# First values kind by kind, softplus on GpSimd, and four tables of a two-layer trunk a tick later

## The chip, the core and the metric

The kernel runs on one core of a Trainium2 chip. A core has five engines that run side by side, each with its own stream of instructions: TensorE (PE) multiplies matrices, VectorE (DVE) works on vectors, ScalarE (ACT) evaluates functions and copies, GpSimd (POOL) does small work and issues some transfers, and SyncE (SP) issues the others. They are tied by semaphores: an instruction waits until what it reads is written. The metric is the device time of one execution in microseconds (us). Lower is better.

## What is computed

Two layers, each with a residual sum and a LayerNorm, on 512 tokens of width 1024, all in float32. The first ("even") layer feeds two branches from one input projection; the second ("odd") is differential attention. Cut to its steps, the reference is:

```python
# even layer
q, k, v, g_ret, xb, g_lru = split(x @ w_in)
q, k = rope(q), rope(k) * 128 ** -0.5
ret = retention(q, k, v)                     # 8 heads of 128, causal, decaying per head
ret = group_norm(ret) * gn_g + gn_b          # per head
ret = ret * silu(g_ret)
xc = causal_conv4(xb) + conv_b
r, i = sigmoid(xc @ wa + ba), sigmoid(xc @ wx + bx)     # 8 diagonal blocks of 128
log_a = -8 * r * softplus(-lam)
h = scan(a=exp(log_a), u=xc * i * sqrt(1 - exp(2 * log_a)))
y = concat(ret, h * silu(g_lru)) @ w_out
x = layer_norm(alpha * x + y)
# odd layer, 8 heads of two maps each
p = softmax(causal(q @ k.T))                 # rope on q and k; 16 maps
o = (p[map 0] - lam * p[map 1]) @ v          # values 256 wide
o = o * rsqrt(mean(o ** 2) + eps) * subln_g * (1 - lambda_init) * silu(g)
x = layer_norm(alpha * x + o @ w_out)
```

## The kernel before

Every operand of a large product is held as two parts, a high half and a low half: ACT casts the float32 value to the matmul's type (`h`), and DVE subtracts that from the value to get the rest (`l`). `split` (L146) does both. A product is three matmuls, here called kinds: high by high, high by low, low by high (`mm3`, L155). Each is 128 by 128 by up to 512 columns, and sums into a bank of PSUM. Weights come through `fetch` (L171): SP issues the transfer of 128 rows by 1024 columns into a raw buffer, which is then split; the names in the profile are `w0_r`, `w0h`, `w0l` and so on, numbered in the order of use. The raw buffers are few, so a later transfer waits until an earlier split is done.

PE and SP run in the order in which the program is written. The order on ACT, DVE and POOL is made by a scheduler when the kernel is built; `tc.high_priority(n)` raises an instruction by `n`, and `keep_in_program_order` pins one.

The program is a row of large units (values, gates, queries and keys, output), whose matmuls fill PE. Beside them run small jobs: the retention of a head, a block of the recurrence, a block of 128 queries of attention, LayerNorm. Each is a generator. After each triple of matmuls the large unit calls `side.tick()`; a job that has yielded `n` goes on `n` ticks later, and then puts its own few matmuls into PE's stream. The tables at the top of the program (L28 to L38) hold these delays. `RET_SCORES` and `RET_NORM` are those of a head of retention before its next score block and before its group norm, `LRU_GATES` that of a block of the recurrence before its gates, `ATT_TURN` that of attention between the transposes of its weights and their product with the values, by block of queries, and `ATT_NORM` that between this product and the transposes of its normalised result `o`.

These are the places that the change touches, and what stands there.

- *The first unit*, `v_even(0)` through `s_unit` (L206): the values of the first half of the heads, in four blocks of 128 tokens (`sb`), each with its own bank (`ev_ps`), over 8 slices of the contraction (`kt`), two to each of the weights w0 to w3. Block by block it does the three kinds of one slice, then of the other; for w0 it does all blocks of the first slice ahead of the second. x itself arrives in pieces, split by ACT and DVE (`xh`, `xl`), and w0 in two halves. A filler matmul on constants (L320) stands behind the very first one. When the last slice of a block is done, `evac` (L450) takes the mean of each head off: a reduce, a small scaling and a subtract on DVE (L454, L455, L457), then a split. The next unit, `gl0`, begins in the bank of block 0.
- *Softplus* (L422 to L440): 23 steps on 128 by 8 numbers, one of them a reciprocal, all on DVE. The result (`sp`) is first read by ACT in the gates of block 0 of the recurrence (L535).
- *A head of retention* (L467): four score blocks (`rs`), each multiplied by the decay (`rsd`) and split (`r00h` and so on: head, block), then their product with the values (`ro`), its square (`rq`), and the sum of it over the head by ones (`rv`). The score blocks have a priority of `P_SCORES` = 13, the rotation of queries and keys (`rope`, L343) one of `P_ROPE` = 50.
- *Attention* (L645): scores (`as`), mask and maximum on DVE (`nm`), exponential on ACT (`e`, L658), transposes (`wt`), split (`w33h`: head and block), the product with the values (`po`), its sum of squares on ACT (L691), the root on GpSimd (L694, L363), `o` on DVE (L697), transposes of it back into the same bank (L701), and a split (`om`). The product takes a bank of its own or borrows one of the large units; `own` says which. While a unit of gates and values runs, `busy[0]` is 1; while a query or key unit runs, `spare[0]` is set.
- *A unit of gates and values* (`gates_values`, L777) uses four banks, `one` (`gv2a` in the second such unit) and `two` (`gv2b`). It multiplies into `one`, then into `two`; half way through the latter, ACT copies `one` out (L799, names `p`), and the unit goes on summing into `one` (L156, right operand `sx`).

## Time and profile before

| | us |
|---|---|
| median of 3 runs | 925.92 (925.37 to 926.28) |
| the profiled execution, its own time | 926.56 |
| span of its profile | 924.8 |
| PE busy | 907.1 (98%) |
| DVE busy | 743.9 (80%) |
| ACT busy | 478.1 (52%) |
| POOL busy | 104.5 (11%) |

The granted clock of TensorE is 0.997 of full speed. Matmuls are pipelined: one of 512 columns is drawn 0.39 us long, and the next begins 0.23 us after it. So a pause of PE is read from the start of one matmul to the start of the next. A wait view gives for each engine what it waited for, in all, how often, and the longest; a row of a timeline gives start, length, engine, line, operation and operands, and in brackets the idle time ahead of it with its releaser.

### The profile page before, as it was taken

The numbers are of one execution on the slowest core, as the hardware profiler recorded it, in microseconds if no ns is written. First come the engines' busy times: TensorE is split into PE (matmuls) and PEld (weight loads), VectorE is DVE, ScalarE is ACT, GpSimd is POOL, SyncE is SP. The second block draws the span as 40 slices with busy tenths as digits, with TensorE's granted clock in tenths as the row PEclk, the third lists the DMA queues.
The fourth block names the chain that finished last, engine by engine and source line by source line (L and its number), as shares of the span: only waits on it lengthen the run. The fifth ranks groups of instructions, "written<-read, shape, count | busy, mean of one in ns | idle before, by whom it ended". The sixth has DMA issues, their size and how long they took to land.

```text
span 924.8 us, 11823 instructions
## 1 busy us (share of the span) xinstructions
PE 907.1 (98%) x4257; PEld 750.3 (81%) x4257; DVE 743.9 (80%) x1244; ACT 478.1 (52%) x779; POOL 104.5 (11%) x167
## 2 busy tenths in 40 slices
PE   8999999999999999999999999999999999999996
PEld 6888888888888878888888888888888888788885
DVE  5977987959768988897888897759868678868787
ACT  5567787557474668532424456433456333664340
POOL 0120010110102010010101210000120100201122
PEclk9999999999999999999999999999999999999998
DMA  7895463862929371534842226546237382277102
GB/s 251 276 314 150 122 169 108 261 183 58 289 57 280 92 193 61 179 117 151 331 167 69 69 68 246 210 163 245 72 130 253 141 318 87 74 258 265 48 1 91
DMA packets 46522, 152.92 MB, mean 165 GB/s; under 512 B 6144, under 2 KB 6272, under 8 KB 45696
## 3 DMA queue, kind: packets, MB, share of 16 engines
q1 hardware_dynamic: 41472, 135.39, 41.4%
q0 software_dynamic: 4992, 16.78, 9.4%
q8 instruction: 33, 0.54, 0.2%
q14 instruction: 25, 0.20, 0.1%
HBM read 139.57 MB, written 37.75 MB: 192 GB/s over the span
## 4 chain that ended last, share of the span: by engine, by line
PE 73%; DVE 14%; ACT 5%; issue 3%; POOL 3%; DMA 1%; SPq 0%; DVEq 0%; ACTq 0%; POOLq 0%
PE oo_ps L159 2%; PE oo_ps L156 2%; PE oo_ps L158 2%; PE out_ps L156 2%; PE out_ps L159 2%; PE out_ps L158 2%; ACT e L658 1%; PE gr_ps L159 1%; PE gr_ps L158 1%; PE gr_ps L156 1%; PE gl_ps L156 1%; PE gl_ps L159 1%; PE gl_ps L158 1%; POOL ave L694 1%; DMA w_r<-in_ev_w 1%
## 5 line engine op out<-in xcount | busy, mean ns | idle before, releaser
L658 ACT ACTIVATE e<-as,nm 128x128 f32<-128x128 f32 (+3 forms) x64 | 33.2, 524 | 42.5 <-DVE nm L655 42.4
L697 DVE SCALAR_TENSOR_TENSOR o<-po,ars,og 128x256 f32<-128x256 f32 x32 | 15.5, 484 | 36.5 <-POOL ars L363 36.4
L665 POOL TENSOR_SCALAR zr<-z 128x1 f32<-128x1 f32 x32 | 14.9, 466 | 259.2 <-ACT e L658 259.2
L187 POOL DMA_DIRECT2D t<-t x24 | 18.8, 784 | 159.0 <-DMA t<-in_od_w 154.6
L187 POOL DMA_DIRECT2D t<-in_od_w x24 | 19.0, 792 | 146.5 <-DMA t<-in_od_w 146.5
L694 POOL TENSOR_SCALAR ave<-ss,zr 128x1 f32<-128x1 f32 x32 | 17.9, 559 | 133.9 <-ACT po L691 133.2
L655 DVE CUSTOM_DVE_ANT_0 as<-as,mask 128x128 f32<-128x128 f32 (+3 forms) x64 | 30.3, 510 | 1.4 <-PE as L159 1.4
L691 ACT ACTIVATE po<-po 128x256 f32<-128x256 f32 x32 | 11.9, 373 | 30.9 <-PE po L159 30.8
L536 DVE TENSOR_TENSOR xbp<-xbp,xc 128x512 f32<-128x512 f32 x8 | 5.5, 691 | 18.4 <-ACT xbp L533 18.4
L363 POOL TENSOR_TENSOR ars<-ave,nhalf 128x1 f32<-128x1 f32 x32 | 19.5, 608 | 2.7
L666 DVE SCALAR_TENSOR_TENSOR e<-e,zr,e 128x128 f32<-128x128 f32 (+3 forms) x32 | 17.6, 550 | 0.8
L519 DVE SCALAR_TENSOR_TENSOR xc<-xbp,vecs,xc 128x509 f32<-128x509 f32 (+2 forms) x24 | 17.9, 747 | 0.1
L262 DVE TENSOR_TENSOR y<-oo_ps,y 128x512 f32<-128x512 f32 x24 | 16.0, 685 | 2.2 <-PE oo_ps L159 2.1
L475 DVE TENSOR_TENSOR rsd<-rs,dec 128x512 f32<-128x512 f32 (+3 forms) x32 | 15.6, 488 | 2.7 <-PE rs L159 2.7
L363 POOL TENSOR_TENSOR lrs<-lve,nhalf 128x1 f32<-128x1 f32 x8 | 7.3, 909 | 84.4 <-DVE lve L376 84.4
L701 PEld LDWEIGHTS po<-ident,o 128*128 128x128 f32 x64 | 8.6, 141 | 7.3 <-DVE o L697 3.8
L701 PE MATMUL po<-ident,o 128*128 128x128 f32 x64 | 12.5, 276 | 1.8 <-DVE o L697 1.8
L670 PE MATMUL wt<-ident,e 128*128 128x128 f32 x80 | 13.9, 272 | 0.0
L528 ACT ACTIVATE t<-pr,vecs 128x512 f32<-128x512 f32 x8 | 5.5, 688 | 15.8 <-PE pr L159 15.8
L663 DVE RECIPROCAL zr<-z 128x1 f32<-128x1 f32 x32 | 5.2, 162 | 10.3 <-ACT e L658 9.9
L670 PEld LDWEIGHTS wt<-ident,e 128*128 128x128 f32 x80 | 10.5, 141 | 3.5
L152 ACT CAST hh<-ht 128x512 fp32r<-128x512 f32 x8 | 4.7, 586 | 15.8 <-PE ht L615 15.8
(2846 smaller groups left out, 3474.5 us busy)
## 6 DMA issues: line engine op xcount, KB each, us to landing
w_r<-in_od_w SPq DMA_DIRECT2D x58, 512.0 KB, 5.6
w_r<-in_ev_w SPq DMA_DIRECT2D x47, 512.0 KB, 5.4
t<-in_od_w SPq DMA_DIRECT2D x48, 256.0 KB, 5.8
sx<-sd SPq DMA_DIRECT2D x24, 512.0 KB, 5.7
w_r<-t SPq DMA_DIRECT2D x24, 512.0 KB, 3.3
w_r<-in_ev_wo SPq DMA_DIRECT2D x16, 512.0 KB, 5.3
w_r<-in_od_wo SPq DMA_DIRECT2D x16, 512.0 KB, 4.0
t<-in_od_w POOLq DMA_DIRECT2D x24, 256.0 KB, 5.0
```

The lines of the kernel that those rows point to most:

```text
L156: nc.tensor.matmul(out=out, lhsT=l[0], rhs=r[0], start=start, stop=False, **kw)
L158: nc.tensor.matmul(out=out, lhsT=l[0], rhs=r[1], start=False, stop=False, **kw)
L159: nc.tensor.matmul(out=out, lhsT=l[1], rhs=r[0], start=False, stop=stop, **kw)
L187: nc.gpsimd.dma_start(out=dst, in_=two, max_dma_last_dim=4 * D, accum_op=ALU.add)
L363: nc.gpsimd.tensor_tensor(out=out, in0=var, in1=nhalf[:, :1], op=ALU.pow)
L519: nc.vector.scalar_tensor_tensor(out=xc[:, sh:], in0=xb[:, :S - sh], scalar=conv_w(w, c), in1=xc[:, sh:], op0=ALU.mult, op1=ALU.add)
L655: nc.vector.tensor_tensor_reduce(out=ps[:, :n], in0=ps[:, :n], in1=mask[:, S - n:], scale=-QK_SCALE, scalar=3.0e38, op0=ALU.add, op1=ALU.m ...
L658: nc.scalar.activation(out=e, in_=ps[:, :n], func=AF.Exp, scale=-1.0, bias=nm, accum_out=z[:, mp:mp + 1])
L666: nc.vector.scalar_tensor_tensor(out=ee[0], in0=ee[1], scalar=zr[:, 0:1], in1=ee[0], op0=ALU.mult, op1=ALU.add)
L670: nc.tensor.transpose(out=pt[:, kb * P:kb * P + P], in_=ee[0][:, kb * P:kb * P + P], identity=ident)
L694: nc.gpsimd.tensor_scalar(out=ve, in0=ss, scalar1=zr[:, 1:2], scalar2=None, op0=ALU.add)
L701: nc.tensor.transpose(out=pm[:, i * P:i * P + P], in_=o[:, i * P:i * P + P], identity=ident)
```

## The change

The first four weights (w0 to w3) are multiplied kind by kind: for a slice, one kind for all four blocks, then the next kind. The filler matmul is gone. The first half of w0 is cast by DVE and not by ACT. All of softplus but the reciprocal moves from DVE to GpSimd, with the last step cut in two. The last score block of a head gets the priority `P_SQUARE` = 60, above the rotation. Heads 1 and 3 wait one tick more before their group norm, block 2 of the recurrence one more before its gates, the last block of queries one more before its product with the values. Between this product and the transposes of `o`, one tick more is waited for where `spare[0]` is set; elsewhere the delay is `ATT_NORM + busy[0]`.

```diff
@@ -27,12 +27,12 @@
 
 RET_START = (13, 13, 13, 13, 13, 13, 13, 8)
 RET_SCORES = (4, 4, 4, 7)
-RET_NORM = (8, 6, 8, 6, 8, 6, 5, 5)
-LRU_GATES = (12, 12, 12, 12, 12, 12, 9, 12)
+RET_NORM = (8, 7, 8, 7, 8, 6, 5, 5)
+LRU_GATES = (12, 12, 13, 12, 12, 12, 9, 12)
 LN_TURN = 15
 ATT_START, ATT_GAP = (12,) * 7 + (7,), (8,) * 7 + (7,)
 ATT_SCORES = (7, 7, 7, 9)
-ATT_TURN = (4, 3, 4, 4)
+ATT_TURN = (4, 3, 4, 5)
 ATT_NORM = 5
 ATT_VALUE, GV_VALUE = 2, 4
 ATT_FREE, ATT_LENT = 2, 8
@@ -143,20 +143,18 @@
     def cut(t, *ix):
         return t[0][ix], t[1][ix]
 
-    def split(src, dst, scale=None):
+    def split(src, dst, scale=None, copy=nc.scalar.copy):
         if scale is not None:
             s = sg[:, scale:scale + 1]
             nc.scalar.activation(out=dst[0], in_=src, func=AF.Identity, scale=s)
             nc.vector.scalar_tensor_tensor(out=dst[1], in0=src, scalar=s, in1=dst[0].bitcast(F32), op0=ALU.mult, op1=ALU.subtract)
             return
-        nc.scalar.copy(out=dst[0], in_=src)
-        nc.vector.tensor_tensor(out=dst[1], in0=src, in1=dst[0].bitcast(F32), op=ALU.subtract)
-
-    def mm3(out, l, r, start, stop, between=lambda: None, **kw):
-        nc.tensor.matmul(out=out, lhsT=l[0], rhs=r[0], start=start, stop=False, **kw)
-        between()
-        nc.tensor.matmul(out=out, lhsT=l[0], rhs=r[1], start=False, stop=False, **kw)
-        nc.tensor.matmul(out=out, lhsT=l[1], rhs=r[0], start=False, stop=stop, **kw)
+        copy(out=dst[0], in_=src)
+        return nc.vector.tensor_tensor(out=dst[1], in0=src, in1=dst[0].bitcast(F32), op=ALU.subtract)
+
+    def mm3(out, l, r, start, stop, kinds=range(3), **kw):
+        for n in kinds:
+            nc.tensor.matmul(out=out, lhsT=l[n == 2], rhs=r[n == 1], start=start and n == 0, stop=stop and n == 2, **kw)
 
     def load(name, shape, src, pl=None, tag=None, bufs=None):
         t = (pl or const).tile(shape, F32, tag=tag or name, name=name, bufs=bufs)
@@ -177,7 +175,7 @@
             for lo, hi in parts:
                 c = slice(lo, hi)
                 nc.sync.dma_start(out=raw[:, c], in_=src[:, c])
-                split(raw[:, c], cut(w, ALL, c), scale=scale)
+                split(raw[:, c], cut(w, ALL, c), scale=scale, copy=nc.vector.tensor_copy if n == 0 and lo == 0 else nc.scalar.copy)
                 yield
             for then in behind.pop(n, ()):
                 then()
@@ -204,13 +202,13 @@
         return ps
 
     def s_unit(act, name, major, evac, before=None):
-        def product(ps, w, sb, kt):
+        def product(ps, w, sb, kt, kinds=range(3)):
             j = kt % 2 * HALF
-            between = {"between": lambda: busy_pe(2)} if (taken[0], sb, kt) == (1, 0, 0) else {}
-            mm3(ps, cut(act, ALL, kt, slice(sb * P, sb * P + P)), cut(w, ALL, slice(j, j + HALF)), kt == 0, kt == KT - 1, **between)
-            if kt == KT - 1:
-                evac(sb, ps)
-            side.tick()
+            mm3(ps, cut(act, ALL, kt, slice(sb * P, sb * P + P)), cut(w, ALL, slice(j, j + HALF)), kt == 0, kt == KT - 1, kinds)
+            if 2 in kinds:
+                if kt == KT - 1:
+                    evac(sb, ps)
+                side.tick()
 
         if major:
             with tc.high_priority(P_WEIGHTS):
@@ -224,12 +222,16 @@
             ps = [bank(ps_pj, "pj", f"{name}_ps{sb}") for sb in range(SB)]
             for i in range(KT // 2):
                 w = take(2)
-                steps = [(sb, j) for sb in range(SB) for j in range(2)]
-                if taken[0] == 1:
-
-                    steps.sort(key=lambda t: t[1])
-                for sb, j in steps:
-                    product(ps[sb], w, sb, 2 * i + j)
+                if taken[0] <= KT // 2:
+
+                    for j in range(2):
+                        for n in range(3):
+                            for sb in range(SB):
+                                product(ps[sb], w, sb, 2 * i + j, (n,))
+                    continue
+                for sb in range(SB):
+                    for j in range(2):
+                        product(ps[sb], w, sb, 2 * i + j)
 
     def out_unit(mix, y, name, first, before=None, after=None, late=0, early=0, apart=False):
         n = len(mix)
@@ -328,13 +330,15 @@
     halves = fetch(((0, HALF), (HALF, D)))
     for n, (lo, hi) in enumerate(((0, 1), (1, 2), (2, 4), (4, 6), (6, 8))):
         nc.sync.dma_start(out=xr[:, lo:hi], in_=a["xt"][:, lo:hi])
+        if n == 0:
+            next(halves)
         for kt in range(lo, hi):
-            split(xr[:, kt], cut(x, ALL, kt))
-        if n < 2:
-            next(halves)
-            if n == 1:
-                list(halves)
-        elif n < 4:
+            low = split(xr[:, kt], cut(x, ALL, kt))
+            if n == 0:
+                tc.keep_in_program_order(low)
+        if n == 1:
+            list(halves)
+        elif 1 < n < 4:
             list(fetch())
 
     nhalf = const.tile([P, SB], F32, tag="nhalf", name="nhalf")
@@ -426,18 +430,19 @@
     lam = vecs[:, 7]
     nc.scalar.activation(out=sa, in_=lam, func=AF.Abs)
     nc.scalar.activation(out=sa, in_=sa, func=AF.Exp, scale=-1.0)
-    nc.vector.tensor_scalar(out=sb_, in0=sa, scalar1=2.0, scalar2=None, op0=ALU.add)
+    nc.gpsimd.tensor_scalar(out=sb_, in0=sa, scalar1=2.0, scalar2=None, op0=ALU.add)
     nc.vector.reciprocal(out=sb_, in_=sb_)
...
-    nc.vector.scalar_tensor_tensor(out=sp4, in0=sb_, scalar=4.0, in1=sc, op0=ALU.mult, op1=ALU.add)
+        nc.gpsimd.tensor_tensor(out=sc, in0=sc, in1=sb_, op=ALU.mult)
+        nc.gpsimd.tensor_scalar(out=sc, in0=sc, scalar1=1.0 / n, scalar2=None, op0=ALU.add)
...
+    nc.gpsimd.tensor_scalar(out=sb_, in0=sb_, scalar1=4.0, scalar2=None, op0=ALU.mult)
+    nc.gpsimd.tensor_tensor(out=sp4, in0=sb_, in1=sc, op=ALU.add)
 
     def silu(ps, out, name):
         s = work(name + "_sg")
@@ -470,7 +475,7 @@
             n = S - jb * P
             ps = bank(ps_sc, "sc", f"rs{h}{jb}")
             mm3(ps[:, :n], cut(k, ALL, slice(jb * P, jb * P + P)), cut(q, ALL, slice(jb * P, S)), True, True)
-            with tc.high_priority(P_SCORES):
+            with tc.high_priority(P_SCORES if jb < SB - 1 else P_SQUARE):
                 s = temp(f"rsd{h}{jb}")
                 nc.vector.tensor_tensor(out=s[:, :n], in0=ps[:, :n], in1=dec[:, :n], op=ALU.mult)
                 t = part(n, f"r{h}{jb}")
@@ -695,7 +700,7 @@
             rsqrt(ve, rs)
             o = es.tile([P, 2 * P], F32, tag="o", name=f"o{hd}{qb}")
             nc.vector.scalar_tensor_tensor(out=o, in0=po[:, :2 * P], scalar=rs, in1=gates[qb, hd // 2][:, hc:hc + 2 * P], op0=ALU.mult, op1=ALU.mult)
-        yield ATT_NORM + max(not own, busy[0])
+        yield ATT_NORM + max(1 + (not own) if spare[0] else 0, busy[0])
         pm = po[:, 2 * P:]
         for i in range(2):
             nc.tensor.transpose(out=pm[:, i * P:i * P + P], in_=o[:, i * P:i * P + P], identity=ident)
```

The order of the instructions shows it at three places. On PE, at the beginning of the first V unit, the order was this (the names are bank, weight, and part of x; `ev_ps_245` and on are the banks of the four blocks):

```order
L156 MATMUL ev_ps_245<-w0h,xh 128x512
L321 MATMUL idle<-ones 128x256
L158 MATMUL ev_ps_245<-w0l,xh 128x512
L159 MATMUL ev_ps_245<-w0h,xl 128x512
L156 MATMUL ev_ps_246<-w0h,xh 128x512
L158 MATMUL ev_ps_246<-w0l,xh 128x512
L159 MATMUL ev_ps_246<-w0h,xl 128x512
L156 MATMUL ev_ps_247<-w0h,xh 128x512
```

and now it is this, with the banks `ev_ps_246` to `_249`:

```order
L157 MATMUL ev_ps_246<-w0h,xh 128x512
L157 MATMUL ev_ps_247<-w0h,xh 128x512
L157 MATMUL ev_ps_248<-w0h,xh 128x512
L157 MATMUL ev_ps_249<-w0h,xh 128x512
L157 MATMUL ev_ps_246<-w0l,xh 128x512
L157 MATMUL ev_ps_247<-w0l,xh 128x512
L157 MATMUL ev_ps_248<-w0l,xh 128x512
L157 MATMUL ev_ps_249<-w0l,xh 128x512
L157 MATMUL ev_ps_246<-w0h,xl 128x512
L157 MATMUL ev_ps_247<-w0h,xl 128x512
L157 MATMUL ev_ps_248<-w0h,xl 128x512
L157 MATMUL ev_ps_249<-w0h,xl 128x512
```

The three kinds of one bank stood together; now each kind runs over the four banks before the next one begins.

On DVE, behind the first V unit, the group means of the four blocks stood apart, with the split of w6 and of the values themselves between them:

```order
L153 TENSOR_TENSOR w4l<-w_r,w4h 128x1024
L153 TENSOR_TENSOR w5l<-w_r,w5h 128x1024
L454 TENSOR_REDUCE vm<-ev_ps_245 128x4
L455 TENSOR_SCALAR vm<-vm 128x4
L457 TENSOR_TENSOR vc<-ev_ps_245,vm 128x512
L454 TENSOR_REDUCE vm<-ev_ps_246 128x4
L153 TENSOR_TENSOR w6l<-w_r,w6h 128x1024
L153 TENSOR_TENSOR ev00l<-vc,ev00h 128x512
L455 TENSOR_SCALAR vm<-vm 128x4
L454 TENSOR_REDUCE vm<-ev_ps_247 128x4
```

and now stand together behind w6:

```order
L153 TENSOR_TENSOR w5l<-w_r,w5h 128x1024
L153 TENSOR_TENSOR w6l<-w_r,w6h 128x1024
L459 TENSOR_REDUCE vm<-ev_ps_246 128x4
L459 TENSOR_REDUCE vm<-ev_ps_247 128x4
L460 TENSOR_SCALAR vm<-vm 128x4
L153 TENSOR_TENSOR gw0l<-gw_437,gw0h 128x512
L460 TENSOR_SCALAR vm<-vm 128x4
L462 TENSOR_TENSOR vc<-ev_ps_246,vm 128x512
L462 TENSOR_TENSOR vc<-ev_ps_247,vm 128x512
L459 TENSOR_REDUCE vm<-ev_ps_248 128x4
```

The subtract of block 0 (`vc` of the first bank), which frees the bank, stood directly behind its own reduce and scaling; now a second reduce, a second scaling and the split `gw0l` stand between.

On ACT, in the second unit of gates and values, the two copies out of `gv2a` stood ahead of the cast of w117 and of the next head's exponentials (`e`):

```order
L152 CAST w116h<-w_r 128x1024
L691 ACTIVATE po_6188,ss<-po_6188 128x256
L799 COPY p_6215<-gv2a_6099 128x512
L799 COPY p_6217<-gv2a_6100 128x512
L152 CAST w117h<-w_r 128x1024
L658 ACTIVATE e_6235,z<-as_6229,nm 128x128
L658 ACTIVATE e_6243,z<-as_6237,nm 128x128
L774 ACTIVATE p_6215<-og_6272 128x512
```

and now stand behind them, the second one behind `om3h` too:

```order
L152 CAST w116h<-w_r 128x1024
L696 ACTIVATE po_6179,ss<-po_6179 128x256
L152 CAST w117h<-w_r 128x1024
L663 ACTIVATE e_6222,z<-as_6216,nm 128x128
L663 ACTIVATE e_6230,z<-as_6224,nm 128x128
L804 COPY p_6237<-gv2a_6099 128x512
L152 CAST om3h<-po_6179 128x2x128
L804 COPY p_6239<-gv2a_6100 128x512
L152 CAST w33h<-wt_6260 128x512
```

The square of `po` keeps its place behind w116h; the copies have moved past the cast of w117 and two exponentials.

More of the change, by code (lines that the diff above doesn't have):

```diff
@@ L428, in trunk @@
     nc.scalar.activation(out=sa, in_=sa, func=AF.Exp, scale=-1.0)
-    nc.vector.tensor_scalar(out=sb_, in0=sa, scalar1=2.0, scalar2=None, op0=ALU.add)
+    nc.gpsimd.tensor_scalar(out=sb_, in0=sa, scalar1=2.0, scalar2=None, op0=ALU.add)
     nc.vector.reciprocal(out=sb_, in_=sb_)
-    nc.vector.tensor_tensor(out=sa, in0=sa, in1=sb_, op=ALU.mult)
-    nc.vector.tensor_tensor(out=sb_, in0=sa, in1=sa, op=ALU.mult)
-    nc.vector.tensor_scalar(out=sc, in0=sb_, scalar1=1.0 / 17, scalar2=1.0 / 15, op0=ALU.mult, op1=ALU.add)
+    nc.gpsimd.tensor_tensor(out=sa, in0=sa, in1=sb_, op=ALU.mult)
+    nc.gpsimd.tensor_tensor(out=sb_, in0=sa, in1=sa, op=ALU.mult)
+    nc.gpsimd.tensor_scalar(out=sc, in0=sb_, scalar1=1.0 / 17, scalar2=1.0 / 15, op0=ALU.mult, op1=ALU.add)
     for n in (13, 11, 9, 7, 5, 3, 1):
-        nc.vector.tensor_tensor(out=sc, in0=sc, in1=sb_, op=ALU.mult)
-        nc.vector.tensor_scalar(out=sc, in0=sc, scalar1=1.0 / n, scalar2=None, op0=ALU.add)
-    nc.vector.tensor_tensor(out=sc, in0=sc, in1=sa, op=ALU.mult)
-    nc.vector.tensor_scalar(out=sb_, in0=lam, scalar1=-1.0, scalar2=0.0, op0=ALU.mult, op1=ALU.max)
-    nc.vector.tensor_scalar(out=sc, in0=sc, scalar1=8.0, scalar2=None, op0=ALU.mult)
-    nc.vector.scalar_tensor_tensor(out=sp4, in0=sb_, scalar=4.0, in1=sc, op0=ALU.mult, op1=ALU.add)
+        nc.gpsimd.tensor_tensor(out=sc, in0=sc, in1=sb_, op=ALU.mult)
+        nc.gpsimd.tensor_scalar(out=sc, in0=sc, scalar1=1.0 / n, scalar2=None, op0=ALU.add)
+    nc.gpsimd.tensor_tensor(out=sc, in0=sc, in1=sa, op=ALU.mult)
+    nc.gpsimd.tensor_scalar(out=sb_, in0=lam, scalar1=-1.0, scalar2=0.0, op0=ALU.mult, op1=ALU.max)
+    nc.gpsimd.tensor_scalar(out=sc, in0=sc, scalar1=8.0, scalar2=None, op0=ALU.mult)
+    nc.gpsimd.tensor_scalar(out=sb_, in0=sb_, scalar1=4.0, scalar2=None, op0=ALU.mult)
+    nc.gpsimd.tensor_tensor(out=sp4, in0=sb_, in1=sc, op=ALU.add)
     def silu(ps, out, name):
```

## The prediction, as it was made before the run

> **What bounds the kernel now.** I read the head of the page first, to see which engine's time the span is.
>
> ```profile
> span 924.8 us, 11823 instructions
> PE 907.1 (98%) x4257; PEld 750.3 (81%) x4257; DVE 743.9 (80%) x1244; ACT 478.1 (52%) x779; POOL 104.5 (11%) x167
> ```
>
> TensorE (PE) is busy for 98% of the span, and the change takes away a single matmul of 4257. It can only win the moments in which PE stands still. So the second view is that of the waits, for PE alone:
>
> ```profile
> PE po L701 <- DVE o L697: 1.8, 4, 0.5
> PE ro L158 <- DVE r63l L153: 1.2, 1, 1.2
> PE ev_ps L156 <- ACT w0h L152: 0.7, 2, 0.5
> PE po L156 <- DVE om1l L153: 0.6, 1, 0.6
> PE ev_ps L158 <- DVE w1l L153: 0.5, 1, 0.5
> PE pr L158 <- DVE xc2l L153: 0.4, 1, 0.4
> PE po L159 <- DVE w03l L153: 0.4, 1, 0.4
> PE ro L158 <- DVE r53l L153: 0.4, 1, 0.4
> PE po L159 <- DVE w33l L153: 0.3, 1, 0.3
> PE po L159 <- DVE w53l L153: 0.3, 1, 0.3
> PE ev_ps L158 <- DVE w3l L153: 0.3, 1, 0.3
> PE rv L493 <- DVE rq3l L153: 0.2, 1, 0.2
> PE rv L493 <- DVE rq1l L153: 0.2, 1, 0.2
> ```
>
> Each of these rows is something that the change moves. They add up to 7.3 us, under 1% of the span. That understates them, as PE's timeline shows:
>
> ```profile
> 29.73 0.39 PE L159 MATMUL ev_ps<-w3h,xl 128*128 128x512 f32 x1
> 29.96 0.39 PE L156 MATMUL gl_ps<-xh,w4h 128*128 128x512 f32 x1
> 341.32 0.22 PE L156 MATMUL ro<-r63h,ev13h 128*128 128x128 f32 x1
> 342.76 0.33 PE L158 MATMUL ro<-r63l,ev13h 128*128 128x128 f32 x1 [1.22 <-DVE r63l L153]
> ```
>
> Matmuls of 512 columns start 0.23 us apart although each is drawn 0.39 long, so part of a standstill lies under the drawn end of the matmul before it. I therefore measure a stall from start to start, less the pitch (0.06 for these 128 columns, a quarter of 0.23): r63l costs 342.76 − 341.32 − 0.06 = 1.38. The first matmul after a stall is also slow by about 0.11 (0.33 against 0.22 here). A stall that is wholly removed is thus worth about 0.3 more than its row.
>
> **The first V unit.** These are its rows in order of time, from the timeline, the last from the chain of waits:
>
> ```profile
> 8.20 0.62 ACT L152 CAST w0h<-w_r 128x512 fp32r<-128x512 f32 x1 [1.68 <-DMA w_r<-in_ev_w]
> 8.87 0.49 PE L156 MATMUL ev_ps<-w0h,xh 128*128 128x512 f32 x1 [0.15 <-ACT w0h L152]
> 18.94 0.17 DVE L429 TENSOR_SCALAR sb__218<-sa 128x8 f32<-128x8 f32 x1
> 19.35 1.05 ACT L152 CAST w3h<-w_r 128x1024 fp32r<-128x1024 f32 x1 [1.19 <-DMA w_r<-in_ev_w]
> 23.34 1.22 DVE L153 TENSOR_TENSOR w3l<-w_r,w3h 128x1024 fp32r<-128x1024 f32 x1
> 24.61 0.50 PE ev_ps L158
> ```
>
> The cast of w0's first half on VectorE (DVE), beside ScalarE's (ACT) cast of x, saves at most the 0.62 by which ACT does one after the other, and the missing filler matmul some 0.2. But the first half of w0 is only 12 matmuls, about 2.8 us, and its second half lands at 8.2 and is cast until 8.8. PE waits there in any case: I put both at nothing, with −0.8 as the lower bound if the landing came sooner.
>
> Kind by kind, PE does four matmuls with w1's high half before it needs the low one, not one. The low half is no sooner there, but three more matmuls lie ahead of it: 3 × 0.23 = 0.68 off the w1l wait (0.5, and 0.3 hidden). Softplus, which stood on DVE from 18.94 until w3l at 23.34, is gone from DVE: w3l then follows its cast at about 20.4 (19.35 + 1.05), and the wait at 24.61 (0.3 idle and 0.25 hidden, 0.56) goes. The last V matmul would end 0.68 + 0.56 = 1.2 us sooner.
>
> That is not what the next unit waits for. Its first matmul writes the bank of V's block 0, which is free only when DVE has done the group means of that block:
>
> ```profile
> 26.75 0.68 DVE L454 TENSOR_REDUCE vm<-ev_ps 128x4 f32<-128x512 f32 x1
> 27.46 0.17 DVE L455 TENSOR_SCALAR vm<-vm 128x4 f32<-128x4 f32 x1
> 27.67 0.69 DVE L457 TENSOR_TENSOR vc<-ev_ps,vm 128x512 f32<-128x512 f32 x1
> L153 DVE TENSOR_TENSOR gw0l<-gw,gw0h 128x512 fp32r<-128x512 f32 x1 | 0.7, 685 | 0.0
> ```
>
> Before, block 0 ends 18 matmuls ahead of the unit's last, and its three DVE steps lie under the other blocks. Kind by kind, the four blocks end within 0.9 us. DVE's new order behind them is reduce, reduce, small, gw0l, small, subtract: with starts 0.60 apart (a 0.68 or 0.69 row hides 0.08 of the next), 2 × 0.60 + 0.07 + 0.60 + 0.07 + 0.69 = 2.6 us. The unit's matmuls would end at 29.96 − 1.24 = 28.7, block 0's last, three earlier, near 28.2, so its bank is free near 30.9, while the next unit began at 29.96 (first row of gl_ps above). **+1.0** is my term. The ends are −1.2 (the bank is in time after all) and +3.0 (w6's split falls among these steps: its 1.22, and its cast at a late landing).
>
> **Softplus on GpSimd.** 23 ops of 128x8 are added there. The nearest rows are small ones on that engine, and ACT's first use of the result:
>
> ```profile
> L694 POOL TENSOR_SCALAR ave<-ss,zr x32: 295/297/1841, 495.8 to 903.9; 128x1 f32<-128x1 f32 x32
> L535 ACT ACTIVATE t<-t,sp x8: 714/727/727, 51.3 to 348.0; 128x512 f32<-128x512 f32 x8
> ```
>
> At the median and about 0.1 between them, 23 × 0.4 = 9 us from 19 is done at 28, far ahead of 51.3. At the longest, 23 × 1.84 = 42 us: done at 61, ACT stuck 10 us. I take the median, hence **0**; the long value is one of 32.
>
> [...]
>
> **The even layer's ticks.** A tick is one triple of matmuls, 3 × 0.23 = 0.68 us. One tick more puts 0.68 of other work before a stage. The stalls, each its row plus 0.3 (0.15 for the short r53l): xc2l 0.7, rq1l 0.5, rq3l 0.5, r53l 0.55. The gates' tick leaves about 0.2 of the first, with the slow first matmul: **−0.5**. Heads 1 and 3 get one tick before their norm: 0.68 covers 0.5, **−0.5** each. The last score block ahead of the rope lets r53l go in front: **−0.55**.
>
> ```profile
> 341.21 0.69 DVE L153 TENSOR_TENSOR xc7l<-xc,xc7h 128x512 fp32r<-128x512 f32 x1
> 342.42 0.28 DVE L153 TENSOR_TENSOR r63l<-rsd,r63h 128x128 fp32r<-128x128 f32 x1
> L158 PE MATMUL pr<-xc7l,gw6h x1: 392/392/392, 345.4 to 345.4; 128*128 128x512 f32 x1
> ```
>
> r63l moves ahead of the rope of q too and its 1.38 goes. In exchange xc7l falls behind the rope, w57l and q7l on DVE: from 341.9 to about 344.5. PE wants it at 345.4, but comes 1.4 sooner now, near 344.0: a wait of about 0.45 is new. **−0.9**. What moves in this layer gives −0.5 − 0.5 − 0.5 − 0.55 − 0.9 = −2.95. If nothing is late in exchange it is −3.4 (all of r63l); if the ticks only shift the waits, nothing.
>
> **The attention's ticks.** A stage waits one tick longer between a block's product and its transposes (only while a query or key unit runs) and before the last block's product. That meets three gates-and-values units, alike in pattern; here the second:
>
> ```profile
> 672.38 1.06 ACT L799 COPY p<-gv2a 128x512 f32<-128x512 f32 x2
> 674.94 0.48 DVE L697 SCALAR_TENSOR_TENSOR o<-po,ars,og 128x256 f32<-128x256 f32 x1 [0.77 <-POOL ars L363]
> 677.27 0.36 ACT L658 ACTIVATE e<-as,nm 128x128 f32<-128x128 f32 x1
> 677.72 0.47 PE L156 MATMUL gv2a<-w114h,sx 128*128 128x512 f32 x1
> 681.94 0.38 PE L159 MATMUL po<-ov10h,w33l 128*128 128x256 f32 x1 [0.30 <-DVE w33l L153]
> ```
>
> Removed here are the wait for o (the row of L701: 1.8 for four, 0.45 each and 0.25 hidden, 0.7) and that for w33l (0.30 and 0.25 hidden, 0.55): 1.25. But now ACT copies the first product out of its bank (L799) behind the exponentials of the next head, which end at 677.6, where before it copied by 673.4. They cannot go earlier, since their scores' maxima stand behind o on DVE, and o waits for GpSimd at 674.94. The first copy (0.53) ends near 678.2, and the matmul at 677.72 must wait for it, as it adds into that bank. Whatever PE won ahead of this is lost here, and 0.5 more; the 0.55 of w33l behind it stays won: about **−0.1**, twice (the second and third unit). The ends: −1.25 if the copy is in time, +1.4 if it is 1.5 later than I work out. In the first unit some 3 us of waits go (o twice, w03l, om1l), but its window is the one where DVE is full:
>
> ```profile
> 490.00:520.00 30.00, 29.57 (x154) 24.70 (x153) 26.17 (x54) 12.34 (x33) 4.97 (x10) 1.00 0.18 59
> ```
>
> 26.17 of 30 us, and the same copies and w03l, w11l and om1l come out late against a PE that is early. I take **0** (−3 to +1.5).
>
> **The sum.** V unit +1.0, even layer −2.95, attention −0.2: −2.15. On the profiled execution's 926.56 that is 924.4; the median of the runs shown, 925.92, lies 0.64 under the profiled one, so **923.8**.
>
> **Rivals.**
> 1. *Nothing takes the place of the attention's waits* (all rows of o, w03l, om1l, w33l and w53l go with their hidden part). 3.0 + 2 × 1.25 instead of 0.2, 5.5 at the most; in part made up for by DVE, thus some 3 to 5 us better: 919 to 921. For it: DVE is at 80%, ACT at 52%. Against it: the order of ACT's copies.
> 2. *The starts of stages shift, the waits follow.* The even ticks bring half of 2.95 and the attention nothing: 923.8 + 1.5 + 0.2 = 925.5, no change to be told. For it: PE is at 98%, so it reaches the next late operand as much sooner. Against it: r63l and the two norms have no operand behind them that is as late.
> 3. *Slower: the copies on ACT.* The mechanism of the attention part, priced higher. It starts to cost where the first copy ends later than PE arrives (677.0 with the won 0.7). I have 678.2; if GpSimd's chain ahead of o takes the long value (1.84 for 0.30) or the exponentials come a score block later, it is 1.5 later in each of three units: +4.5, 923.8 + 4.5 = 928.3. Against it: one row of 32 is that long.
> 4. *Softplus comes late.* Each op on GpSimd at the long value, done at 61: ACT, in order, stands from 51.3 to 61. PE runs on for the 12 ticks (8.2 us) by which the gates of the recurrence trail their block, and loses the other 2: 923.8 + 2 = 925.8. For it: the maximum of 1841. Against it: the median of 297.
>
> **How the numbers follow.** The forecast 0.50, the first rival 0.20, the second 0.14, the third 0.13, the fourth 0.03. What a measurement of this kernel can tell is 0.2%, 1.85 us: faster is under 924.1, slower over 927.8. The forecast lies 0.3 under the first border, so I give 0.35 of its 0.50 to faster and 0.15 to no change; with the rivals faster 0.35 + 0.20 = 0.55, same 0.15 + 0.14 + 0.03 = 0.32, slower 0.13. The likeliest case's own range is 922 to 925.5; to hold 8 in 10 the range takes in most of the first rival and all of the second and fourth, 919.5 to 926.8, and leaves out the third.
>
> **What would show it.** In the changed profile: r63l, r53l, rq1l and rq3l gone from PE's waits; a wait of the unit behind V on DVE's subtract of block 0, its first matmul near 30.9; w3l on DVE near 20.4 and softplus on GpSimd ended before 35; new waits on a copy of ACT in the gates-and-values units. I am wrong if softplus reaches the tanh at 51.3, if the first unit behind V starts before 30.1, or if o and the w waits of the attention go without a wait on a copy, om or o in their place.

## The result, and the profile after

| | before | changed |
|---|---|---|
| median | 926.03 us (925.31 to 926.72, 12 runs) | 928.08 us (926.20 to 930.63, 12 runs) |
| ratio | | 1.0022 (95%: 1.0013 to 1.0031) |
| profiled execution | 926.56 us | 926.57 us |
| span of its profile | 924.8 us | 924.8 us |

The change makes the kernel 0.22% slower, where 0.23% faster was forecast. Two things strike at once. The profiled executions are equal to a hundredth of a microsecond, so the trace of the changed kernel shows neither a loss nor the gain that was forecast; the loss is in its other executions. And these spread over 4.4 us, where the kernel before stays within 1.4.

First, then, the profiled execution. These are TensorE's waits in it, to be set against those of before in the prediction (`...` marks rows that are left out):

```profile
PE gl_ps L157 <- DVE vc L462: 2.6, 1, 2.6
...
PE gv1a L157 <- ACT p L804: 0.7, 1, 0.7
PE po L157 <- ACT w03h L152: 0.5, 1, 0.5
PE out_ps L157 <- ACT xc L521: 0.5, 1, 0.5
PE po L157 <- DVE w11l L153: 0.5, 1, 0.5
PE po L706 <- DVE o L702: 0.4, 2, 0.2
PE pr L157 <- DVE xc7l L153: 0.4, 1, 0.4
...
PE out_ps L157 <- DVE gl L450: 0.3, 1, 0.3
PE gv3a L157 <- ACT p L804: 0.3, 1, 0.3
PE gv2a L157 <- ACT p L804: 0.3, 1, 0.3
...
PE ev_ps L157 <- ACT w0h L152: 0.3, 1, 0.3
PE rs L157 <- DVE rsd L480: 0.2, 1, 0.2
```

The old rows of r63l, r53l, rq1l, rq3l, xc2l, w1l and w3l are gone, as the change meant. In their place stands the bank of V's block 0 (`vc`), the largest wait of the kernel. Below it are ACT's copies in the units of gates and values (`p`), and three rows that nothing in the prediction speaks of: `xc`, `gl` and `rsd`.

To see what each place is worth, take the start of the first matmul with a given weight in both traces. At all these places the same matmuls lie ahead in both, but for the one filler.

| place (first matmul with the weight) | before, us | changed kernel against it |
|---|---|---|
| V unit over (w4) | 29.96 | +1.57 |
| behind xc2l's gates and head 1's norm (w19) | 126.27 | +0.51 |
| past 141 to 146 us (w25) | 164.87 | +2.61 |
| (w51) | 326.13 | +1.31 |
| even layer's last stages (w54) | 349.11 | +0.53 |
| attention begun (w81) | 512.57 | −0.11 |
| attention nearly over (w156) | 869.09 | +0.23 |
| end of the span | 924.76 | +0.01 |

Behind the V unit 1.1 us were won by 126 us, 2.1 lost again by 165, 2.1 won by 349, and 0.5 more from there to the end: together they just make good the V unit's 1.57.

### The profile page after: what moved, and what is told of

The parts are those of the page before. It is cut to its first block, busy times and chain, and to the rows that moved or that the text cites. A ratio compares the mean times of both kernels' runs of the same rounds, so it can differ in the third digit from the quotient of the medians.

```text
span 924.8 us, 11834 instructions
## 1 busy us (share of the span) xinstructions
PE 907.2 (98%) x4256; PEld 750.4 (81%) x4256; DVE 740.8 (80%) x1223; ACT 478.3 (52%) x779; POOL 114.9 (12%) x190
## 4 chain that ended last, share of the span: by engine, by line
PE 84%; DVE 7%; ACT 3%; DMA 2%; issue 2%; POOL 1%; SPq 0%; DVEq 0%; ACTq 0%; POOLq 0%
PE oo_ps L157 7%; PE gr_ps L157 5%; PE out_ps L157 4%; PE q_ps L157 4%; PE gl_ps L157 4%; PE k_ps L157 4%; PE xb_ps L157 4%; PE po L157 3%; PE as L157 3%; PE gv2a L157 2%; PE ov_ps L157 2%; PE gv3a L157 2%; PE ev_ps L157 2%; PE eo_ps L157 2%; PE og_ps L157 2%; DMA w_r<-in_ev_w 2%
## 5 line engine op out<-in xcount | busy, mean ns | idle before, releaser
L670 POOL TENSOR_SCALAR zr<-z 128x1 f32<-128x1 f32 x32 | 16.9, 528 | 246.9 <-ACT e L663 246.9
L660 DVE CUSTOM_DVE_ANT_0 as<-as,mask 128x128 f32<-128x128 f32 (+3 forms) x64 | 30.5, 507 | 2.6 <-PE as L157 2.6
```

The source lines that it names most:

```text
L660: nc.vector.tensor_tensor_reduce(out=ps[:, :n], in0=ps[:, :n], in1=mask[:, S - n:], scale=-QK_SCALE, scalar=3.0e38, op0=ALU.add, op1=ALU.m ...
L670: nc.gpsimd.tensor_scalar(out=zr[:, 1:2], in0=z[:, 0:1], scalar1=z[:, 0:1], scalar2=EPS, op0=ALU.mult, op1=ALU.mult)
```

## The experiments

Two theories were on the table. The *order theory* says that the loss is the sum of TensorE's standstills, each set by an order on DVE or ACT. The *clock theory* adds that the standstill behind the V unit also lowers TensorE's granted clock in most executions, which the one profiled execution happens not to show.

### The changed kernel again

No edit: the changed kernel, run beside the next three.

> The changed kernel once more, unaltered. Its profiled execution had a span of 924.8 us at a mean granted clock of 0.998, while its median lay 1.5 us above that execution, with lower mean clocks (0.993 to 0.996). Clock theory: the 2.6 us standstill of TensorE behind the first V unit lets the granted clock fall in some executions, for about 3 to 4 us at half speed (0.002 of 925 us at half is 3.7 us, 1.85 us lost); executions differ by 1.5 to 4 us, and a profiled one at 0.996 shows a clock below 1.00 in the windows just behind 31 us. Rival: the slower executions lose time elsewhere (late transfers), and the clock at 25 to 40 us is 1.00 in all. Median 927.5 to 928.5 us by both.

928.24 us median (926.28 to 928.83); ratio 1.0017 (1.0008 to 1.0026). The profiled execution was again one of the short ones (926.28 us, clock 0.998, wait of 2.5 us at `gl_ps`), so its trace could not decide. The spread repeats. The mean clocks of all 23 executions of the two runs go with their times: six at 0.998 took 926.2 to 926.7 us, the other 17, at 0.993 to 0.997, took 927.4 to 930.6. (3.4 us at half speed lower the mean over 925 us by 0.0018.) The next two runs, meant for other questions, show the place.

### The gates of block 2 at 12 ticks, and attention as before

```diff
-LRU_GATES = (12, 12, 13, 12, 12, 12, 9, 12)
+LRU_GATES = (12, 12, 12, 12, 12, 12, 9, 12)
```

> As changed, but the gates of block 2 of the recurrence wait 12 ticks again. Theory from the trace: the 13th tick let ACT's activation on the second gate fall behind the square of a head, with two more table loads, and the recurrence's end came 7.6 us later on DVE; TensorE then stood three times between 141 and 145 us (1.6 us, 2.0 with the slow first matmuls). Without the tick these three waits go and the old one at xc2l (0.7) comes back: 1.3 us shorter than the changed kernel. Rival: the tick of the group norm of head 1 does it, and the waits at 141 to 145 stay: no change, or 0.6 longer. The spread between executions stays as in the changed kernel by both.

```diff
-ATT_TURN = (4, 3, 4, 5)
+ATT_TURN = (4, 3, 4, 4)
...
-        yield ATT_NORM + max(1 + (not own) if spare[0] else 0, busy[0])
+        yield ATT_NORM + max(not own, busy[0])
```

> As changed, but both attention delays are as before. In the traces the changed kernel is 0.1 us ahead behind the even layer (at 512 us) and level at the end: the attention delays bring waits of the same sum. So the profiled execution is 0 to 0.5 us shorter than that of the changed kernel, and the median the same within 0.5 us if the spread comes from the V unit; if the attention's waits made the clock fall, the spread goes here and the median falls by 1.5 us.

Gates: 927.94 us (926.58 to 929.72), ratio 1.0019 (1.0010 to 1.0027). Attention: 928.90 us (926.94 to 929.26), ratio 1.0026 (1.0017 to 1.0035). Both still spread like the changed kernel, and both profiled executions were long ones. The view by windows gives, for each stretch, its length, the busy times of PE, its weight loads, DVE, ACT and POOL (in brackets the number of instructions), then TensorE's granted clock, and last the share and rate of the transfers. First the changed kernel, whose profiled execution was short:

```profile
28.00:32.00 4.00, 1.41 (x7) 0.89 (x6) 4.00 (x9) 1.97 (x3) 3.00 (x4) 1.00 0.93 349
32.00:34.00 2.00, 2.00 (x11) 1.65 (x10) 2.00 (x6) 1.58 (x3) 0.77 (x1) 1.00 1.03 242
34.00:36.00 2.00, 2.00 (x11) 1.65 (x10) 2.00 (x4) 0.87 (x2) 0.00 (x0) 1.00 1.05 195
```

and then the one with the gates at 12 ticks, whose V unit is the same:

```profile
28.00:32.00 4.00, 1.82 (x9) 1.22 (x8) 4.00 (x9) 1.98 (x4) 3.29 (x6) 1.00 0.93 365
32.00:34.00 2.00, 2.00 (x7) 1.59 (x6) 2.00 (x6) 1.39 (x2) 0.80 (x1) 0.53 1.06 234
34.00:36.00 2.00, 2.00 (x7) 1.54 (x7) 2.00 (x4) 1.06 (x2) 0.00 (x0) 0.61 0.99 178
```

The clock falls to a half for 3.4 us, from 0.8 us after TensorE has resumed. PE reads as busy in both (2.00 of 2.00), so busy time tells nothing here; the count of matmuls does, 7 against 11. Its timeline shows it in the pitch:

```profile
31.34 0.47 PE L157 MATMUL gl_ps<-xh,w4h 128*128 128x512 f32 x1 [2.18 <-DVE vc L462]
31.64 0.40 PE L157 MATMUL gl_ps<-xl,w4h 128*128 128x512 f32 x1
...
32.93 0.63 PE L157 MATMUL gl_ps<-xh,w4l 128*128 128x512 f32 x1
33.35 0.63 PE L157 MATMUL gl_ps<-xh,w4h 128*128 128x512 f32 x1
33.78 0.63 PE L157 MATMUL gl_ps<-xl,w4h 128*128 128x512 f32 x1
```

The starts are 0.43 apart there and 0.23 elsewhere: eight matmuls at 0.2 more are 1.6 us. From the first matmul with w4 to the first with w5 this execution loses 1.71 us against the kernel before, and the one with the attention as before 1.71 too; the changed kernel's profiled execution loses 0.08. So in these two executions the clock falls where the clock theory says, and it costs 1.7 us; that the standstill causes it is for the runs further down to show.

What the two edits themselves do is read from the traces, since the clock's drop is in both. Without the tick of the gates the waits at 141 to 146 us are gone, as expected, and xc2l's comes back; but a wait for k2l, which neither kernel has, is new and was not expected:

```profile
PE rs L157 <- DVE k2l L153: 0.7, 1, 0.7
PE pr L157 <- DVE xc2l L153: 0.6, 1, 0.6
```

From w5 to w54 it gains 1.43 us against the kernel before, the changed kernel 1.12: the tick costs 0.3 us, not the expected 1.3. With the attention as before the run gains 0.1 us from w54 to the end (+2.61 to +2.52), the changed kernel 0.5 (+0.53 to +0.01): the attention's delays are worth 0.4 us in the traces, where none was expected. The medians agree in sign (928.90 against 928.24, a little over the 0.5 us up to which they were to be the same).

### w3 block by block

```diff
-                if taken[0] <= KT // 2:
+                if taken[0] < KT // 2:
```

> As changed, but w3 is multiplied block by block again (w0, w1 and w2 stay kind by kind), so that block 0's bank has its last matmul 18 matmuls ahead of the unit's last. Order theory: the wait of 2.6 us at the next unit shrinks to under 1 us (block 0's subtract stands behind the split of w6, which ends near 28.9), the next unit begins near 29.5 instead of 31.5, and the profiled execution is 2 us shorter than that of the changed kernel (926.57), near 924.5. Clock theory: beside this the spread between executions goes (all within 1 us) and the mean clock is 0.998, so the median falls by 3 to 4 us from 928.1, to 924 to 925. If the clock has nothing to do with that wait, the median falls by 2 us only, and the spread stays.

924.54 us (923.71 to 925.33), ratio to the kernel before 0.9980 (0.9971 to 0.9989): 3.7 us below the changed kernel on the same chip. Its profiled execution gains 1.44 us (924.84 against 926.28), so over half of the fall in the median is what no profiled execution of the changed kernel showed; the mean clock is 0.997 or 0.998 in every execution. The remaining wait was 1.5 us, not under 1, since block 0's subtract stood on DVE behind block 1's reduce and the split of w6:

```profile
27.91 1.23 DVE L153 TENSOR_TENSOR w6l<-w_r,w6h 128x1024 fp32r<-128x1024 f32 x1 [1.40 <-ACT w6h L152]
29.05 0.68 DVE L462 TENSOR_TENSOR vc<-ev_ps,vm 128x512 f32<-128x512 f32 x1
```

DVE waited 1.40 us for w6 with the subtract ready behind it: the order was fixed when the kernel was built, and w6's transfer was late for it.

### Filler matmuls in the standstill

This is meant to change nothing but TensorE's idleness: nine matmuls on constants between the V unit and the next.

```diff
+                    if taken[0] == KT // 2:
+                        spot = bank(ps_tp, "tp", "spot")
+                        for _ in range(9):
+                            busy_pe(4, spot)
                     continue
```

> The changed kernel with nine filler matmuls on constants (nine times 0.23 = 2.05 us) between the first V unit and the next; the orders of DVE, ACT and POOL are those of the changed kernel, row for row. The work waited for is as late as before, so the next unit begins near 31.5 us as in the changed kernel; only TensorE is not idle for 2.6 us but for 0.6. Clock theory: the drop of the granted clock seen at 32 to 36 us (two profiled executions, 1.7 us lost) goes, the mean clock is 0.998 in all, and the median falls from 928.2 to 926.3 +- 0.4 us, that is to the times of the executions without the drop. Rival (the drop has another cause, such as the transfers at that place): the median stays at 928.

926.62 us (925.62 to 927.37), ratio 1.0006 (0.9997 to 1.0015), against 928.08 and 928.24 for the changed kernel. Work that computes nothing makes it 1.5 us faster, with the same transfers and the same orders on DVE, ACT and GpSimd, and the mean clock is 0.997 or 0.998 in all 11 executions. In its profile the clock is 1.00 behind the V unit:

```profile
28.00:31.00 3.00, 2.91 (x13) 2.16 (x12) 3.00 (x8) 1.57 (x2) 0.79 (x1) 1.00 1.00 302
31.00:35.00 4.00, 4.00 (x19) 3.28 (x19) 4.00 (x9) 2.46 (x5) 0.77 (x1) 1.00 1.05 271
```

The profiled execution itself is no measure of it: there the next unit began at 30.5 and not at 31.5, as w6 happened to land a microsecond sooner. The mean clock of 0.997 in some executions, this one among them, was not the 0.998 that I expected of all; the end of the program, where TensorE runs out of work and the clock falls too (at 918.07 us here, at 920.88 in the changed kernel), enters it.

### The kind-by-kind order alone

The kernel before, with w0 to w3 kind by kind and no filler at the start; softplus, casts and tables as before:

```diff
-                steps = [(sb, j) for sb in range(SB) for j in range(2)]
...
+                if taken[0] <= KT // 2:
+                    for j in range(2):
+                        for n in range(3):
+                            for sb in range(SB):
+                                product(ps[sb], w, sb, 2 * i + j, (n,))
+                    continue
```

> The kernel before with one part of the change alone: w0 to w3 kind by kind and no filler matmul (softplus on DVE, all casts on ACT, all tables as before). My account: the four blocks end together near 29.3 us, w6's split stands ahead of their reduces on DVE and ends near 30.2 (its transfer is released by w3's late split), and block 0's subtract ends near 32.9. TensorE stands still for 3 us or more, the next unit begins 2.5 to 3 us later than in the kernel before, and in most executions the granted clock drops behind it (1.7 us more): span 927.5 to 929.5, median 928.5 to 930.7. Rival (the loss of the changed kernel needs another of its parts too): the next unit begins no more than 1 us later, the clock stays, median under 927.3.

931.87 us (930.52 to 933.40), ratio 1.0065 (1.0050 to 1.0080), 1.2 us above the range that I gave. Its wait is 3.9 us, and the clock drops to half behind it:

```profile
PE gl_ps L157 <- DVE vc L459: 3.9, 1, 3.9
```

```profile
32.00:34.00 2.00, 1.10 (x3) 0.94 (x4) 2.00 (x6) 1.96 (x3) 0.80 (x1) 0.77 1.01 395
34.00:36.00 2.00, 2.00 (x6) 1.54 (x6) 2.00 (x6) 1.16 (x3) 0.77 (x1) 0.50 1.08 277
36.00:38.00 2.00, 2.00 (x10) 1.63 (x9) 2.00 (x4) 1.16 (x2) 0.00 (x0) 0.88 1.02 231
```

One part of the change alone costs 5.7 us; the others, which bring w6 a microsecond sooner (its split began at 28.62 here and at 27.62 in the changed kernel) and win waits further on, hid most of that.

### All but the kind-by-kind order

The reverse: the changed kernel with w0 to w3 block by block as before.

```diff
-                if taken[0] <= KT // 2:
...
+                steps = [(sb, j) for sb in range(SB) for j in range(2)]
+                if taken[0] == 1:
+                    steps.sort(key=lambda t: t[1])
+                for sb, j in steps:
+                    product(ps[sb], w, sb, 2 * i + j)
```

> As changed, but w0 to w3 block by block as before (softplus on GpSimd, w0's first half cast by DVE and all tables stay as changed). Softplus' place on DVE gives 0.56 us (w3l's wait), the even layer and the attention 1.6 us by the comparison of the traces, the V unit loses nothing and the clock does not drop: 926.2 - 2.2 = 924.0 us (923.6 to 924.6). If the cast by DVE or GpSimd's work cost something that the traces hide, 925 or more.

924.25 us (924.04 to 924.66), ratio 0.9980 (0.9971 to 0.9989), within 0.3 us of the sum, and with the spread gone (0.6 us). So softplus on GpSimd and the cast by DVE carry no hidden cost, and the kind-by-kind order is what turned a gain of 1.9 us into a loss of 2. The profiled execution wins 0.75 us up to w4 and 1.7 behind it; the forecast had 3.15 behind it.

### The last score block below the rope

On the basis of the kernel `v_pin` of the next section:

```diff
-            with tc.high_priority(P_SCORES if jb < SB - 1 else P_SQUARE):
+            with tc.high_priority(P_SCORES):
```

> As v_pin, with the last score block of a head at its old priority (below the rope). The waits for r53l (0.54) and r63l (1.37) come back and that for xc7l (0.56) goes: 1.35 us slower than v_pin (923.65), 925.0 +- 0.4. Rival: the trace's gain there came from the other ticks, and nothing changes.

924.66 us (924.18 to 925.10), ratio 0.9982 (0.9973 to 0.9991), 1.0 us above v_pin's 923.65, where 1.35 was expected. The waits moved as expected: r63l and r53l are back, xc7l is gone.

```profile
PE ro L157 <- DVE r63l L153: 1.2, 1, 1.2
PE ro L157 <- DVE r53l L153: 0.4, 1, 0.4
```

### What the pieces give together

V's three DVE steps of each block pinned in the order of the blocks, with w3 block by block (`v_pin`); and, on the basis of `v_rows`, ACT's copies raised in priority and not pinned (`copies2`):

```diff
-                nc.vector.tensor_reduce(out=m, in_=p3, axis=AX.X, op=ALU.add)
+                keep = (lambda t: t) if i else tc.keep_in_program_order
+                keep(nc.vector.tensor_reduce(out=m, in_=p3, axis=AX.X, op=ALU.add))
...
-                tc.keep_in_program_order(nc.scalar.copy(out=ts[n], in_=ps[n]))
+                with tc.high_priority(P_WEIGHTS):
+                    nc.scalar.copy(out=ts[n], in_=ps[n])
```

> As v_rows (w3 block by block), with the reduce, scaling and subtract of the first V unit's blocks pinned on DVE in the order of the blocks, so that block 0's subtract stands ahead of block 1's reduce and of the split of w6. Order theory: the wait of 1.6 us at the next unit, which v_rows still had, is gone (0 to 0.3 left), and the time falls by 1.3 to 1.6 us against v_rows (924.54), to 923.0 to 923.3. Rival: another operand is as late (the split of w5 or the bank of the second unit), and less than 0.7 comes.

> As v_rows, with ACT's copies out of the first bank of the gates-and-values units raised in priority and no longer pinned, so that they stand ahead of the next head's exponentials again. My account of the attention: the waits of TensorE on these copies (0.90, 0.48 and 0.47 us) are gone and little takes their place: 0.8 to 1.5 us shorter than v_rows, 923.0 to 923.7. Rival: TensorE then meets o or om of DVE as late as the copy was, and nothing changes (924.2 to 924.8).

v_pin: 923.65 us (923.35 to 923.70), ratio 0.9971 (0.9960 to 0.9983). The wait behind V is gone, and the next unit starts with no pause:

```profile
25.75 0.69 DVE L463 TENSOR_TENSOR vc<-ev_ps,vm 128x512 f32<-128x512 f32 x1
```

```profile
28.47 0.39 PE L157 MATMUL ev_ps<-w3h,xl 128*128 128x512 f32 x1
28.70 0.39 PE L157 MATMUL gl_ps<-xh,w4h 128*128 128x512 f32 x1
```

The unit starts 1.26 us sooner than in the kernel before. The median gained 0.9 on v_rows, less than the 1.3 to 1.6 expected; the profiled executions differ by 1.22 (the two ran beside the kernel before at 926.16 and 926.25).

copies2: 923.24 us (922.88 to 923.85), ratio 0.9968 (0.9956 to 0.9981), 1.3 below v_rows. The rows of the copies are gone from PE's waits, and part of them went over to `o`, whose row grew from 0.4 for two in the changed kernel to

```profile
PE po L706 <- DVE o L702: 1.1, 3, 0.4
```

Both together, with the gates of block 2 at 12 ticks, and then with head 1's norm at 6 ticks as before too:

> v_pin and copies2 together, with the gates of block 2 of the recurrence at 12 ticks again (worth 0.3 us in the traces). By the sum of the three: 924.5 - 1.5 - 1.2 - 0.3 = 921.5 us (921 to 922.5). If the attention's next waits take the copies' place, 922.7.

> As best, with head 1 waiting 6 ticks before its group norm, as in the kernel before. Best has a wait of 0.85 us for k2l at 134 us that neither the kernel before nor the changed one has; if the moved norm of head 1 causes it, it goes, and rq1l's wait (0.61) comes back: 0.2 us shorter than best (922.03), not told from no change by the times, but seen in the waits. If k2l's wait stays, 0.6 longer.

```diff
-LRU_GATES = (12, 12, 13, 12, 12, 12, 9, 12)
+LRU_GATES = (12, 12, 12, 12, 12, 12, 9, 12)
...
-RET_NORM = (8, 7, 8, 7, 8, 6, 5, 5)
+RET_NORM = (8, 6, 8, 7, 8, 6, 5, 5)
```

best: 922.03 us (921.97 to 922.82), ratio 0.9957 (0.9944 to 0.9969). best2: 921.44 us (921.31 to 921.97), ratio to the kernel before 0.9950 (0.9937 to 0.9962). In the latter k2l's wait is gone and rq1l's is back (0.2 in the wait view), so, with the gates at 12 ticks, k2l's wait comes from the later norm of head 1; the medians differ by 0.6 where 0.2 was expected, which is within what such a comparison tells. best2 is faster than both kernels: 4.75 us below the kernel before, 0.5%. The head of its page:

```profile
span 919.7 us, 11814 instructions
PE 905.4 (98%) x4256; PEld 750.4 (82%) x4256; DVE 741.5 (81%) x1223; ACT 476.5 (52%) x778; POOL 112.9 (12%) x190
```

## Why the prediction was wrong

The forecast was −2.15 us on the profiled execution; it came out at 0.0, and the median at +2.05. Three steps failed. The even layer's ticks were sized at −2.95 and gave −1.1, the V unit at +1.0 and took 1.57; these two, less 0.3 more won in the attention, are the 2.1 us by which the profiled execution missed. The third is the price of a long standstill in the clock behind it, which the prediction put at nothing without a word: 1.7 us in the executions that have it, about 1.5 in the median. By the steps of the prediction:

**The V unit, +1.0: right wait, measured +1.57, with the head of its chain and a consequence left out.** The next unit waited for the bank of block 0, through the order that the prediction reads: reduce, reduce, small, gw0l, small, subtract.

```profile
27.62 1.23 DVE L153 TENSOR_TENSOR w6l<-w_r,w6h 128x1024 fp32r<-128x1024 f32 x1 [2.87 <-ACT w6h L152]
28.76 1.28 DVE L459 TENSOR_REDUCE vm<-ev_ps 128x4 f32<-128x512 f32 x2
29.96 0.16 DVE L460 TENSOR_SCALAR vm<-vm 128x4 f32<-128x4 f32 x1
30.02 0.69 DVE L153 TENSOR_TENSOR gw0l<-gw,gw0h 128x512 fp32r<-128x512 f32 x1
30.63 0.17 DVE L460 TENSOR_SCALAR vm<-vm 128x4 f32<-128x4 f32 x1
30.70 1.28 DVE L462 TENSOR_TENSOR vc<-ev_ps,vm 128x512 f32<-128x512 f32 x2
```

The reduces began at 28.76, not at 28.2. The new order on DVE puts the split of w6 ahead of them, as the listing of that order shows, and DVE stood 2.87 us until w6 was cast; so the chain began at w6's transfer and not at block 0's last matmul. That is the 0.57 by which the term was short; the prediction had this case as its bound of +3.0. The runs with the same order there (the changed kernel again, the gates at 12 ticks, the attention as before) began the unit 1.5, 1.4 and 2.0 us later than before, the one with fillers, where w6 was early, 0.55.

What it missed altogether is that a pause of about 2.6 us was paid for again behind it in most executions. In 17 of the 23 executions time and mean clock tell of a fall, and where a trace shows it, it is to a half (0.50 of full speed) for 3.4 us, 1.7 us more. The rows of the kernel before could not show this: there TensorE never waits more than 1.2 us at a time behind the start and ahead of the end. The term needed a second price: how long is the longest standstill that the change makes, against the longest which the traces show to be harmless. This price turned the median from level to slower; the runs with fillers, with w3 block by block, and without this part show it.

**Softplus on GpSimd, 0: right.** Five of its 23 ops took 0.7 to 1.3 us, the others 0.2 to 0.3, and the last ended at 29.2, long before ACT's first use at 51.3.

```profile
22.44 1.10 POOL L440 TENSOR_SCALAR sc<-sc 128x8 f32<-128x8 f32 x1
...
29.02 0.20 POOL L445 TENSOR_TENSOR sp<-sb__218,sc 128x8 f32<-128x8 f32 x1
```

That is near the median price that the prediction took (done at 28), and far from the longest (done at 61).

**The even layer, −2.95: measured about −1.1** (from +1.65 at w5 to +0.53 at w54). The single terms were there: from w5 to w19 −1.1 (−1.0 forecast for xc2l and rq1l), rq3l −0.7 (−0.5 forecast), r53l and r63l −1.4 (−1.45 forecast, and 1.0 us by the run without the priority), with xc7l's new wait 0.4 as worked out. The step that failed is "one tick more puts 0.68 of other work before a stage". For the gates of block 2 it also reordered ACT: its activation on the second gate fell behind a head's square and a load of an activation table, and needs a load of its own.

```profile
120.27 0.60 ACT L491 ACTIVATE rq<-ro 128x512 f32<-128x512 f32 x1 [0.31 <-PE ro L157]
120.89 1.28 ACT L545 ACT_TABLE_LOAD   x1
...
123.86 1.28 ACT L538 ACT_TABLE_LOAD   x1
125.16 0.69 ACT L538 ACTIVATE xbp<-pi,vecs 128x512 f32<-128x512 f32 x1
...
139.18 1.22 DVE L553 TENSOR_TENSOR_SCAN xc<-t,r 128x512 f32<-128x512 f32 x1
```

In the kernel before, activation and scan stood here:

```profile
117.26 0.69 ACT L533 ACTIVATE xbp<-pi,vecs 128x512 f32<-128x512 f32 x1
...
131.53 1.22 DVE L548 TENSOR_TENSOR_SCAN xc<-t,r 128x512 f32<-128x512 f32 x1
```

The scan came 7.6 us later, and with it the rows `gl`, `rsd` and `xc` of the waits: 1.9 us between 141 and 146, of the 2.1 lost by w25. That the tick causes these waits is shown by the run without it; that it does so through ACT is read from the rows. The prediction did not follow ACT through this stage. The tick cannot be priced alone, though: taken away it gave 0.3 us back, since the tick of head 1's norm then makes TensorE wait for k2l; with both as before (`best2`) the layer gives −1.9 from w5 to w54. My expectation for the gates spoke of two more table loads; the rows count one, seven against six between 110 and 146 us.

**The attention, −0.2: right in mechanism and near in size.** From w54 to the end it is −0.5. The copies are the largest of the waits that took the place of those of o and the weights, and moving them away is worth 1.3 us by the medians, 1.0 by the profiled executions. The rival that priced them at +4.5 did not come.

**The first half of w0, 0: right.** TensorE still waits for the second half at about 8.1 us (`ev_ps <- w0h`, 0.3 in the waits).

Of the rivals, none is what happened. The second, that the waits follow the shifted starts, came near for the even layer (half of 2.95 there, 1.1 measured); the slower one priced ACT's copies, and the loss was at another place and of another kind.

## What to carry to other kernels

A reordering that shortens a matmul unit can lengthen its handover: finishing all banks of a unit together puts the emptying of its banks between it and the next user of the first bank. Where TensorE is 98% busy, ask of each change what its longest standstill will be, not only what the sum of them is, since here pauses of 2.2, 2.7 and 3.9 us were paid for again in the clock behind them, and one of 1.5 us was not. And when a stage is moved by a tick, follow the order on every engine that it issues to, ACT and its table loads (1.28 us each here) too.

## What the runs showed of the hardware

TensorE's granted clock fell to half (0.50) for about 3.4 us behind pauses of 2.2, 2.7 and 3.9 us, 0.8, 1.4 and 0.2 us after TensorE had resumed, and did not in two profiled executions with pauses of 2.6 and 2.5. So in these runs the length of the pause alone did not decide, and one profile can miss what the median pays for. What the falls have in common can be read from the traces. In the kernel before the clock rises at 4.26 us and falls at 919.03, in the changed kernel it rises at 6.11 and falls at 920.88: both times 914.77 us lie between, 268 times 3.413. With the gates at 12 ticks it rises at 4.82, falls at 32.13, rises at 35.54 and falls at 923.01, which is 8, 1 and 260 times 3.413 apart. The times at whole multiples of 3.413 us from a trace's own changes of the clock, here called edges, cut TensorE's pause behind the V unit like this:

| run | pause, us | edge in it | idle ahead of and behind the edge | clock behind |
|---|---|---|---|---|
| changed kernel | 28.94 to 31.53 | 30.00 | 1.06, 1.53 | 1.00 |
| the same again | 28.91 to 31.43 | 30.29 | 1.38, 1.14 | 1.00 |
| w3 block by block | 28.43 to 29.88 | none | 1.46 | 1.00 |
| gates at 12 ticks | 29.16 to 31.34 | none | 2.18 | 0.50 |
| attention as before | 29.26 to 31.98 | 30.00 | 0.74, 1.98 | 0.50 |
| kind by kind alone | 29.00 to 32.90 | 29.67 | 0.67, 3.23 | 0.50 |

In the three of these traces in which the clock fell, TensorE, as they draw it, idled 2.18, 1.98 and 3.23 us between two neighbouring edges, and the clock was at half from the second of them to the next; in the other three it idled at most 1.53 us, and the clock stayed at 1.00. The ends of the programs agree: there 1.93 us of idle time between two edges left the clock at 1.00 (attention as before), and behind 2.05 it fell (`best`). The edges lie elsewhere in each execution (the first rise at 4.26, 4.82 and 6.11 us in the three above), so a pause of 2.6 us can be cut by an edge in one execution and not in another. By these figures, an estimate, with 1.95 taken between the 1.93 and the 1.98, it escapes if an edge falls in its middle 1.3 us (2 × 1.95 − 2.6) of the 3.41, in 4 executions of 10; 6 of the 23 did.
